# Moving the U tiles of a short-convolution layer 32 bytes along in SBUF

## The chip, the cores and the metric

The kernel runs on one core of a Trainium2 chip. The metric is the device time of one launch in microseconds (us). Three runs of the kernel before took 773.32, 773.86 and 774.14 us, with a median of 773.86.

## What is computed

One layer of an encoder trunk (the reference has depth 1, so only its first mixer runs), for 1024 positions of 1024 channels, in float32:

```python
u = rms_norm(h, pre_norm)                        # 1024 x 1024
z, bg, cg, v = split(u @ w_in, 4)                # w_in: 1024 x 8192, four parts of 2048
y = bg * causal_dwconv(cg * v, conv_w) * silu(z) # three taps along the positions
m = y @ w_out                                    # w_out: 2048 x 1024
h = h + rms_norm(m, post_norm)
```

Nearly all of the work is the two matrix products, `u @ w_in` and `y @ w_out`.

## The kernel before

**Precision.** A float32 operand is split into a high part (rounded to the fp32r format) and a low part, what is left of it. A product is then three matmuls per block of the inner dimension: low weights by high input, high weights by low input, high weights by high input (lines 821 to 823, 1425 to 1427 and 1839 to 1841). Every matmul has 128 x 128 weights, loaded just before it, and streams a moving operand of 512 or 256 columns past them. Throughout this document the *moving* operand is the one named first after the arrow in a profile row: `px<-u_d,wdh` streams `u_d` past the weights `wdh` into the PSUM bank `px`.

**Fewer products.** The 2 x 2 blocks of each product are combined in Strassen's manner (Winograd's form): seven block products, named a to g, in place of eight. Three of them, b, f and g, are for most chunks split once more in the same way, into seven smaller products a' to g' whose moving operands have 256 columns. The whole first product runs over 32 pairs p (16 chunks c of 128 output channels, two pairs each); the deep form is used for b in chunks 2 to 15 (14 chunks), for f in 2 to 14 (13), and for g in 2 to 13 (12) (`by_seven`, line 767).

**Where tiles lie.** SBUF is handed out by pools, in the order in which the kernel opens them, one after another and in steps of 32 bytes per partition. In the program before, the pools on which this case turns lie as follows (addresses within a partition):

| pool | what it holds | size of a tile | first address | rest by 64 |
|---|---|---|---|---|
| `up` | the U tiles: 7 slots, used in turn for `u_a` to `u_g`, `xb`, and in the output stage for `ou_*`, `oy_*`, `oA_*`, `oB_*`, `ox_*` | 16,384 | 3,136 | 0 |
| `pages` | 32 pages: raw weights, their sums, their high and low parts (`w*h`, `w*l`, `dw*`), snapshots | 2,048 | 117,824 | 0 |
| `tmp` (opened when the head is done) | `gpad`, 4,104 bytes, takes 4,128 | | 183,360 | 0 |
| `tmp` | `cv`, then 18 slots `u?*_deep` | 4,096; 2,048 | 187,488; 191,584 | 32 |

All slices that a matmul reads begin at multiples of 512 bytes from the start of their tile, so a slice has the same rest by 64 as its tile. So the moving operands of products a to g, and of a', b', e' and f' (slices of `u_b`, `u_f`, `u_g`), begin on a 64-byte line. Those of c', d' and g' are tiles of their own (`deep_split`, line 1347; names `ub?h_deep`, `ub?l_deep` and so on) and begin 32 bytes past one. This comes of the 4,104 bytes of `gpad` alone. All weights begin on a 64-byte line: in the first product they are pages, in the output stage (`out_mm`, line 1831, and `small_mm`, line 1924) they are U tiles, like the moving operands there.

**Order.** Every instruction after the head is recorded first, put into an order by a list scheduler (`Plan.arrange`, line 388) with its own costs for the engines, corrected by a table of hand-set numbers (`PLAN`, line 28), and then issued engine by engine. The order doesn't depend on addresses. TensorE runs the products in the order of `slots` (line 1620): for a pair, c, e, d, the next pair's a, with the deep products of b, f and g between them. ScalarE rounds the high parts and takes snapshots of banks (`snap`, line 827), VectorE makes the low parts and adds, GpSimd makes the sums of weight blocks, SyncE issues the DMAs. After about 615 us comes the output stage: products a to g of `y @ w_out`, 512 columns each but for b and f, which are done in seven of 256 columns; then the last norm and the stores.

All instructions of the profile stand under one line, 252, that of the helper that issues them; tile names tell them apart.

Of the kernel before, what the change touches and what calls it, by code (L numbers as in the profile page):

```python
# [11 lines left out]
F32 = mybir.dt.float32  # L12
# [187 lines left out]
class Op:  # L200

    __slots__ = ("lock", "order", "base", "move", "others", "lead", "est", "engine", "name", "args", "kw", "n", "needs", "feeds", "dur", "lat", "waits", "late", "tiles", "news", "start", "ideal", "pos", "soft")


class Engine:
# [409 lines left out]
def kernel(  # L615
# [35 lines left out]

    const = plan.pool(ctx.enter_context(tc.tile_pool(name="const", bufs=1)), 1)
    small = plan.pool(ctx.enter_context(tc.tile_pool(name="small", bufs=2)), 2)
    up = plan.pool(ctx.enter_context(tc.tile_pool(name="up", bufs=7)), 7)
    pages = plan.pool(ctx.enter_context(tc.tile_pool(name="pages", bufs=PAGES)), PAGES)
    psum = plan.pool(ctx.enter_context(tc.tile_pool(name="psum", bufs=8, space=bass.MemoryType.PSUM)), 8, "psum")
    dram = plan.pool(ctx.enter_context(tc.tile_pool(name="dram", bufs=1, space=bass.MemoryType.DRAM)), 1, "dram")
# [1408 lines left out]
```

## Time and profile before

| | |
|---|---|
| median of three runs | 773.86 us |
| the profiled execution's own time | 772.83 us |
| its span, first to last instruction | 771.0 us |
| mean granted TensorE clock | 0.998 |
| TensorE busy (PE) | 762.2 us, 4320 matmuls |
| VectorE busy (DVE) | 673.9 us |
| ScalarE busy (ACT) | 458.8 us |
| GpSimd busy (POOL) | 462.2 us |

A matmul is pipelined: its recorded duration reaches into the next one. What a matmul costs in a dense row of matmuls is therefore the distance from its start to the next one's start. In the chain of waits, a piece such as "x6" is six matmuls in a row, and its length is the sum of six such distances.

### The profile page before, as it was taken

The numbers are of one execution on the slowest core, as the hardware profiler recorded it, in microseconds if no ns is written. First come the engines' busy times: TensorE is split into PE (matmuls) and PEld (weight loads), VectorE is DVE, ScalarE is ACT, GpSimd is POOL, SyncE is SP. The second block draws the span as 40 slices with busy tenths as digits, with TensorE's granted clock in tenths as the row PEclk, the third lists the DMA queues.
The fourth block names the chain that finished last, engine by engine and source line by source line (L and its number), as shares of the span: only waits on it lengthen the run. The fifth ranks groups of instructions, "written<-read, shape, count | busy, mean of one in ns | idle before, by whom it ended". The sixth has DMA issues, their size and how long they took to land.

```text
span 771.0 us, 12816 instructions
## 1 busy us (share of the span) xinstructions
PE 762.2 (99%) x4320; PEld 669.6 (87%) x4320; DVE 673.9 (87%) x1022; ACT 458.8 (60%) x880; POOL 462.2 (60%) x416
## 2 busy tenths in 40 slices
PE   8999999999999999999999999999999999999996
PEld 7888889898889898888888898988888889889885
DVE  6899988989988978989999989798999898877993
ACT  7765678575656565556556565556653656564831
POOL 2519997889575778696789777584739100600321
PEclk9999999999999999999999999999999999999999
DMA  9222325243333547576858474927465998666842
GB/s 318 66 56 82 119 85 152 101 126 131 97 116 96 171 111 209 126 191 158 239 137 254 116 215 107 249 84 213 122 180 174 335 367 293 197 218 206 274 150 109
DMA packets 117137, 130.11 MB, mean 169 GB/s; under 512 B 7320, under 2 KB 74704, under 8 KB 116944
## 3 DMA queue, kind: packets, MB, share of 16 engines
q1 hardware_dynamic: 112560, 120.77, 49.0%
q0 software_dynamic: 4352, 8.39, 7.1%
q8 instruction: 34, 0.56, 0.3%
q14 instruction: 31, 0.25, 0.1%
q10 hardware_dynamic: 160, 0.14, 0.0%
HBM read 101.74 MB, written 44.30 MB: 189 GB/s over the span
## 4 chain that ended last, share of the span: by engine, by line
PE 98%; DVE 1%; DMA 0%; ACT 0%; POOL 0%; issue 0%; POOLq 0%; ACTq 0%
PE px L252 39%; PE pv L252 15%; PE po_x L252 11%; PE px2b L252 5%; PE px2f L252 4%; PE px2g L252 3%; PE po_v L252 3%; PE pp L252 3%; PE pv2b L252 3%; PE pv2f L252 2%; PE pf_x L252 1%; PE pb_x L252 1%; PE py2b L252 1%; PE pv2g L252 1%; PE py L252 1%; PE pf_v L252 1%
## 5 line engine op out<-in xcount | busy, mean ns | idle before, releaser
L252 PE MATMUL px<-u_d,wdh 128*128 128x512 f32 x248 | 76.8, 390 | 0.0
L252 PE MATMUL px<-u_a,wah 128*128 128x512 f32 x248 | 76.7, 390 | 0.0
L252 PE MATMUL pv<-u_e,weh 128*128 128x512 f32 x248 | 76.7, 390 | 0.0
L252 PE MATMUL px<-u_c,wch 128*128 128x512 f32 x248 | 76.6, 390 | 0.0
L252 ACT COPY beside<-raw 128x512 f32<-128x512 f32 x67 | 39.6, 591 | 31.8 <-DVE wal L252 11.0
L252 PEld LDWEIGHTS px<-u_d,wdh 128*128 128x128 f32 x248 | 46.6, 188 | 9.1
L252 PEld LDWEIGHTS px<-u_c,wch 128*128 128x128 f32 x248 | 46.7, 188 | 9.0
L252 PEld LDWEIGHTS px<-u_a,wah 128*128 128x128 f32 x248 | 46.7, 188 | 8.9
L252 PEld LDWEIGHTS pv<-u_e,weh 128*128 128x128 f32 x248 | 46.6, 188 | 8.9
L252 DVE SCALAR_TENSOR_TENSOR cv<-gpad,cw,cv 128x1024 f32<-128x1024 f32 x32 | 49.7, 1554 | 3.4 <-ACT cv L252 3.3
L252 POOL TENSOR_TENSOR sf<-raw,sc 128x512 f32<-128x512 f32 x30 | 44.5, 1482 | 10.9 <-DVE sc L252 6.0
L252 PE MATMUL px<-u_d,wdl 128*128 128x512 f32 x124 | 48.7, 393 | 0.0
L252 PE MATMUL px<-u_a,wal 128*128 128x512 f32 x124 | 48.7, 393 | 0.0
L252 PE MATMUL px<-u_c,wcl 128*128 128x512 f32 x124 | 48.5, 392 | 0.0
L252 PE MATMUL pv<-u_e,wel 128*128 128x512 f32 x124 | 48.5, 391 | 0.0
L252 POOL TENSOR_TENSOR sc<-se,raw 128x512 f32<-128x512 f32 x25 | 36.5, 1460 | 19.0 <-DVE se L252 10.0
L252 ACT COPY sna<-px 128x512 f32<-128x512 f32 x30 | 17.6, 586 | 49.4 <-PE px L252 47.7
L252 POOL TENSOR_TENSOR raw<-raw,raw 128x512 f32<-128x512 f32 x31 | 44.8, 1446 | 3.3 <-DVE se L252 1.9
L252 POOL TENSOR_TENSOR rs_post<-ve_post,minus_half 128x1 f32<-128x1 f32 x7 | 5.4, 784 | 68.1 <-DVE ve_post L252 68.1
L252 POOL TENSOR_TENSOR se<-raw,raw 128x512 f32<-128x512 f32 x22 | 33.1, 1504 | 17.7 <-DMA raw<-in_sc_w_in 5.7
L252 DVE TENSOR_TENSOR wcl<-sc,wch 128x512 fp32r<-128x512 f32 x31 | 31.6, 1020 | 2.6 <-ACT wch L252 2.6
L252 DVE TENSOR_TENSOR sna<-px2b,sna 128x256 f32<-128x256 f32 x56 | 23.2, 413 | 11.9 <-PE px2b L252 11.9
(486 smaller groups left out, 2637.1 us busy)
## 6 DMA issues: line engine op xcount, KB each, us to landing
raw<-in_sc_w_in SPq DMA_DIRECT2D x128, 256.0 KB, 4.6
y_d<-cv SPq DMA_DIRECT2D x16, 512.0 KB, 3.1
s_d<-s SPq DMA_DIRECT2D x32, 256.0 KB, 4.8
t_d<-in_sc_w_out POOLq DMA_DIRECT2D x16, 512.0 KB, 8.2
tb<-in_sc_w_out SPq DMA_DIRECT2D x16, 256.0 KB, 3.0
t_d<-in_sc_w_out SPq DMA_DIRECT2D x16, 256.0 KB, 4.5
t_d<-t_d SPq DMA_DIRECT2D x16, 256.0 KB, 4.5
s<-y_d SPq DMA_DIRECT2D x16, 256.0 KB, 4.7
```

The source lines that it names most:

```text
L252: getattr(engine, name)(*(self.plain(a) for a in args), **{k: self.plain(a) for k, a in kw.items()})
```

## The change

Two pools of one tile of 32 bytes are opened, one ahead of `up` and one behind it. Nothing reads or writes their tiles.

```diff
+def edge(ctx, tc, name):
+
+    ctx.enter_context(tc.tile_pool(name=name, bufs=1)).tile([128, 8], F32, tag=name, name=name)
...
     small = plan.pool(ctx.enter_context(tc.tile_pool(name="small", bufs=2)), 2)
+    edge(ctx, tc, "edge_u")
     up = plan.pool(ctx.enter_context(tc.tile_pool(name="up", bufs=7)), 7)
+    edge(ctx, tc, "edge_w")
     pages = plan.pool(ctx.enter_context(tc.tile_pool(name="pages", bufs=PAGES)), PAGES)
```

The U tiles then begin at 3,168, 32 bytes past a 64-byte line. The pages and all that lies behind them move by 64 bytes in all, so that their rest by 64 stays: 0 for pages and `gpad`, 32 for `cv` and the deep tiles. No instruction is added, removed or moved to another place in the order.

## The prediction

> **What bounds the kernel.** I read the page first: busy shares, the slices, the chain.
>
> ```profile
> PE 762.2 (99%) x4320; PEld 669.6 (87%) x4320; DVE 673.9 (87%) x1022; ACT 458.8 (60%) x880; POOL 462.2 (60%) x416
> PE   8999999999999999999999999999999999999996
> PE 98%; DVE 1%; DMA 0%; ACT 0%; POOL 0%; issue 0%; POOLq 0%; ACTq 0%
> ```
>
> TensorE is busy in every slice and makes up 98% of the chain that ends last. Nothing else sets the time, so the question is what one matmul costs. The busy time doesn't tell that, since recorded durations overlap; the distance from start to start does. The chain of waits gives it, in pieces (start, length, what, how many matmuls). Here is one stretch of the first product, and the place where the output stage begins:
>
> ```profile
> 303.70 2.75 PE pv L252 x12
> 306.45 0.71 PE pv2b L252 x6
> 307.16 0.72 PE pv2f L252 x6
> 307.88 0.71 PE px2b L252 x6
> 308.59 0.71 PE px2f L252 x6
> ...
> 312.05 0.70 PE px2b L252 x6
> 312.75 0.70 PE pv L252 x6
> 313.45 0.72 PE px L252 x6
> 314.17 0.72 PE px2g L252 x6
> ```
>
> ```profile
> 602.03 2.72 PE pv L252 x12
> 604.75 0.71 PE pv2b L252 x6
> 605.46 0.71 PE px2b L252 x6
> 606.17 2.75 PE px L252 x12
> ...
> 615.09 21.76 PE po_x L252 x96
> 636.85 2.87 PE pb_x L252 x24
> ```
>
> Two things are to be seen. A matmul of 512 columns costs 226.7 ns in a long run (21.76 us for 96; 2.72 for 12). One of 256 costs 120 ns in some pieces (0.72 for six) and 116.7 ns in others (0.70). The timeline tells which are which, around another such place:
>
> ```profile
> 127.29 0.28 PE L252 MATMUL px2b<-ubgh_deep,dwb 128*128 128x256 f32 x1
> ...
> 127.99 0.28 PE L252 MATMUL pv<-ufgh_deep,dwf 128*128 128x256 f32 x1
> ...
> 128.69 0.28 PE L252 MATMUL px<-u_g,dwg0l 128*128 128x256 f32 x1
> ...
> 129.41 0.28 PE L252 MATMUL px2g<-u_g,dwg0l 128*128 128x256 f32 x1
> ```
>
> The twelve from 127.29 to 128.69 us stream deep tiles: 1.40 us, 116.7 ns each. The six from 128.69 to 129.41 stream `u_g`: 0.72 us, 120 ns each. Both have 256 columns and weights out of pages. What differs is the moving tile: the deep tiles begin 32 bytes past a 64-byte line, `u_g` on one. So the kernel before already contains, in small, what the change does to the U tiles, and there the matmul is 3.3 ns cheaper. The groups by form say the same by durations, of matmuls and of weight loads (count, busy, mean ns):
>
> ```profile
> L252 PE MATMUL px2b<-ubgh_deep,dwb 128*128 128x256 f32 x56 | 12.1, 279 | 0.0
> L252 PE MATMUL py2b<-u_b,dwb0h 128*128 128x256 f32 x56 | 10.7, 283 | 0.0
> L252 PEld LDWEIGHTS px2b<-ubgh_deep,dwb 128*128 128x128 f32 x56 | 9.5, 188 | 0.5
> L252 PEld LDWEIGHTS py2b<-u_b,dwb0h 128*128 128x128 f32 x56 | 8.7, 192 | 0.0
> ```
>
> 279 against 283 ns for the matmul, 188 against 192 for the load that runs beside it. Both streams are shorter where the moving tile lies 32 bytes off the weights' rest by 64, which looks like two reads getting in each other's way when they start alike. That is an argument from two numbers, not a proof.
>
> **The change, part by part.** It adds no instruction, wait or DMA and moves none past another. All it can do is change what an instruction costs that reads or writes a U tile.
>
> *Matmuls of 512 columns in the first product.* Their counts come from these groups, where the high weights are two of every three matmuls:
>
> ```profile
> L252 PE MATMUL px<-u_d,wdh 128*128 128x512 f32 x248 | 76.8, 390 | 0.0
> L252 PE MATMUL px<-u_g,wgh 128*128 128x512 f32 x56 | 17.3, 390 | 0.0
> L252 PE MATMUL pv<-u_f,wfh 128*128 128x512 f32 x40 | 12.3, 389 | 0.0
> L252 PE MATMUL py<-u_b,wbh 128*128 128x512 f32 x24 | 7.4, 390 | 0.0
> ```
>
> a, c, d and e have 248 each, so (4 x 248 + 56 + 40 + 24) x 1.5 = 1668, and the plain first pair has eight blocks of 12, 96: 1764. No matmul of 512 columns in this trace streams a tile 32 bytes off, so the gain is unknown. The bounds are nothing and the 4.2 ns that 1.39 in place of the rounded 1.40 us would give the short ones. The nearest row is the 256-column one: 120 - 106.7 = 13.3 ns stand above the 256 / 2.4 ns of the columns themselves, and 226.7 - 213.3 = 13.3 above 512 / 2.4 (2.4 columns a ns is an estimate: 256 more columns cost 226.7 - 120 = 106.7 ns). The same surcharge, independent of length, suggests the same relief. I take 3.3 ns: 1764 x 3.3 = 5.9 us.
>
> *Matmuls of 256 columns that stream U tiles in the first product.* Products a', b', e' and f' of 14 + 13 + 12 = 39 deep forms, six each: 4 x 6 x 39 = 936. `py2b` above has 56 x 1.5 = 84 = 14 x 6, as it should. 936 x 3.3 = 3.1 us, with bounds 2.3 and 3.9 (1.41 and 1.39 us for the twelve).
>
> *Deep tiles that follow U tiles.* At 307.88 and 308.59 they take 0.71 us for six, after U pieces, and at 312.05, after a product of 512 columns, 0.70. If no aligned piece is left, these fall to 0.70: one piece in each of 39 deep forms, 0.01 each, 0.4 us; bounds 0 and 0.8.
>
> *The output stage.* There the weights are U tiles as well. Five products of 96 matmuls of 512 columns and two of 168 with 256 give 816. Weights and moving tile go along together, so their rests by 64 remain alike, as they are today at 226.7 and 120 ns. If two reads that start alike are what costs, nothing changes. Bounds: a gain of 816 x 3.3 = 2.7 us if only the moving tile's start counts, and a loss of 816 x 4 = 3.3 if a shifted weight load is longer by the 4 ns that loads differ in today. The nearest row is today's equal rests, so I take 0.
>
> [...]
>
> *The first matmuls of 512 columns after short ones.* A piece of 12 takes 2.75 us after short pieces (606.17) and 2.72 after long ones (602.03). With eight such pieces in each of 13 chunks that is 104 x 0.03 = 3.1 us. Whether a shifted tile removes it can't be seen: 0 to 3.1 us, and I take 0, because at 606.17 it follows deep tiles that already lie 32 bytes off.
>
> *Writers of U tiles.* The rounding into `u_b` and into a deep tile cost the same:
>
> ```profile
> L252 ACT CAST u_b<-deepb 128x256 fp32r<-128x256 f32 x2 | 0.8, 407 | 0.4 <-PE py L252 0.3
> L252 ACT CAST ubch_deep<-deepb 128x256 fp32r<-128x256 f32 x2 | 0.7, 407 | 0.0
> ```
>
> 407 ns both; I count 0.
>
> *What is late next.* TensorE would run 1.2% faster. VectorE in the middle:
>
> ```profile
> 325.00:405.00 80.00, 80.00 (x480) 71.36 (x479) 72.39 (x107) 44.17 (x85) 60.94 (x58) 1.00 0.66 178
> ```
>
> 72.39 of 80 us is 90%, and becomes about 92%. It keeps up on the average, but has tight places. The tightest I found is a low part of weights, and the tightest that repeats a snapshot of a bank, each followed by the matmul that needs it:
>
> ```profile
> 419.01 0.68 DVE L252 TENSOR_TENSOR wdl<-beside,wdh 128x512 fp32r<-128x512 f32 x1
> ```
>
> ```profile
> 419.89 0.40 PE L252 MATMUL px<-u_d,wdl 128*128 128x512 f32 x1
> ```
>
> ```profile
> 298.20 0.59 ACT L252 COPY sna<-px 128x512 f32<-128x512 f32 x1 [3.44 <-PE px L252]
> ```
>
> ```profile
> 299.37 0.40 PE L252 MATMUL px<-u_c,wcl 128*128 128x512 f32 x1
> ```
>
> 0.20 us and 0.58 us are in hand. Matmuls 3.3 ns cheaper take 0.04 us out of the dozen between snapshot and use, which is nothing; the 0.20 us can be used up where VectorE runs for 0.20 / 0.012, some 17 us, without waiting for TensorE. I charge 0.4 us, with bounds 0 and 2.
>
> The sum is -5.9 - 3.1 - 0.4 + 0.4 = -9.0 us. Against the profiled execution's own 772.83 us that is 763.8. The median of the runs, 773.86, lies 1.03 higher, and it is what is forecast: 764.9.
>
> **The rivals.** *The moving start alone counts.* The output stage gains as well: 764.9 - 2.7 = 762.2. For it: the surcharge of 13.3 ns is as large there as in the first product. Against it: the shorter weight loads.
>
> *Only short matmuls gain.* A matmul of 512 columns leaves 227 ns for a load of 188, a short one only 120; the loads of the short ones overlap the next, and only they might suffer. Then 3.1 + 0.4 = 3.5 us go: 770.4. Against it: the equal surcharge.
>
> *No effect.* The deep tiles also lie elsewhere, above 191,584, the U tiles below 117,824, and the difference could be the region's. Then nothing changes: 773.9. Against it: seven U slots spread over 114,688 bytes show no difference among themselves. [...]
>
> *Slower: the long matmuls settle in a worse rhythm.* After short ones they run slow for half a piece:
>
> ```profile
> 300.76 0.39 PE L252 MATMUL px<-u_c,wcl 128*128 128x512 f32 x1
> ```
>
> From 299.37 to 300.76 are six, 231.7 ns each, 5.0 more than in the long run. Today this dies out. If a shifted tile held it, 1764 x 5.0 = 8.8 us come, 3.5 go: 779.2. It decides from 3.5 / 1764 = 2.0 ns on, a steady distance above 228.7 ns. For it: deep pieces after U pieces do hold their 0.71. Against it: that hold is still below 0.72.
>
> **How the numbers follow.** Forecast 0.43, moving start alone 0.22, short ones only 0.13, no effect 0.10, worse rhythm 0.12. About 0.2%, 1.5 us, is what a measurement of this kernel can tell from no change. Faster: 0.43 + 0.22 + 0.13 = 0.78; same 0.10; slower 0.12. The range takes in the first three cases: low, 762.2 less the 3.1 of the first long matmuls, 759.1; high, 770.4 and a little over for the feeders, 771.0.
>
> **What would show it.** Right: `po_x` still 21.76 us for 96, long pieces of `px` and `pv` in the first product at 2.68 for 12, all deep pieces at 0.70, loads of `py2b` at 188 ns. If `po_x` falls to 21.4, the moving start alone counts. If long pieces stay at 2.72 while short ones fall, the second rival is true; if `py2b` keeps 283 ns, the third. A piece above 2.74 in a long run is the fourth. What would make me wrong without any of these is a wait of TensorE on VectorE or a DMA that isn't in the chain today.

## The result, and the profile after

The changed kernel takes 779.61 us (median of six runs, 779.37 to 780.00), the kernel before 773.90 (six runs, 773.32 to 774.21). The ratio is 1.0075, with a 95% interval from 1.0062 to 1.0088: **slower by 5.7 us**, where 764.9, faster by 9.0, was forecast. The profiled execution took 779.58 us, its span is 777.8, its mean granted TensorE clock 0.999 (before: 772.83, 771.0 and 0.998).

The page of the changed kernel, first the busy times, then the shares of the chain that ends last:

```profile
PE 767.8 (99%) x4320; PEld 667.0 (86%) x4320; DVE 673.3 (87%) x1022; ACT 459.0 (59%) x880; POOL 461.4 (59%) x416
PE 98%; DVE 0%; DMA 0%; ACT 0%; POOL 0%; issue 0%; POOLq 0%; ACTq 0%
```

No new wait is there: TensorE is still 98% of the chain, with as many matmuls. So some of them must have become dearer. Two windows of 500 us, of before and then of after (time, then for each engine its busy time and instructions in the order PE, PEld, DVE, ACT, POOL, then clock, DMA share and GB/s), say so without any durations:

```profile
100.00:600.00 500.00, 500.00 (x2967) 445.00 (x2966) 446.80 (x681) 299.58 (x582) 371.28 (x336) 1.00 0.55 153
```

```profile
100.00:600.00 500.00, 500.00 (x2944) 439.84 (x2943) 442.65 (x675) 297.98 (x580) 366.86 (x336) 1.00 0.54 150
```

At the same clock, 23 matmuls fewer were started in the same time. VectorE had less to do per us, not more.

The chain of waits of the changed kernel, first in the plain first pair, where long pieces follow one another, then at the stretch of the first product and the place that the prediction showed of before:

```profile
74.14 2.80 PE pv L257 x12
76.94 2.80 PE px L257 x12
...
303.48 2.80 PE px L257 x12
306.28 0.70 PE px2f L257 x6
...
621.89 21.76 PE po_x L257 x96
```

Twelve matmuls of 512 columns take 2.80 us, after other long ones (76.94) as well as after short ones (303.48): 233.3 ns each, in place of 226.7. Of the short pieces of this stretch more are at 0.70 than before, and fewer at 0.72. The output stage is as it was, 21.76 us for 96. The groups by form show the same in recorded durations, of matmuls and of a weight load:

```profile
L257 PE MATMUL px<-u_d,wdh 128*128 128x512 f32 x248 | 78.0, 395 | 0.0
L257 PE MATMUL po_x<-ou_d,oy_d 128*128 128x512 f32 x96 | 21.9, 389 | 0.0
L257 PE MATMUL py2b<-u_b,dwb0h 128*128 128x256 f32 x56 | 10.6, 281 | 0.0
```

```profile
L257 PEld LDWEIGHTS py2b<-u_b,dwb0h 128*128 128x128 f32 x56 | 8.5, 188 | 0.0
```

`u_d` against `wdh` went from 390 to 395 ns, `ou_d` against `oy_d` did not move, `u_b` fell from 283 to 281, and its load from 192 to 188.

Summed over the trace, start to start, the matmuls of the two profiled executions account for the time:

| matmuls | count | before, us (mean ns) | after, us (mean ns) | difference |
|---|---|---|---|---|
| first product, U tiles, 512 columns | 1764 | 404.35 (229.2) | 412.32 (233.7) | +7.97 |
| first product, U tiles, 256 columns | 936 | 111.73 (119.4) | 110.75 (118.3) | -0.98 |
| first product, deep tiles, 256 columns | 702 | 82.44 (117.4) | 81.95 (116.7) | -0.49 |
| output stage, 256 columns | 336 | 40.31 (120.0) | 40.30 (120.0) | 0 |
| output stage, 512 columns | 479 | 108.63 (226.8) | 108.63 (226.8) | 0 |

The sum is +6.5 of the 6.8 us by which the span grew; the other 0.3 lie in the warm-up matmuls at the start (7.60 and 7.89 us). The mean of before is 229.2, not 226.7, mostly since pieces of 12 after short ones took 2.75 us; 13 early ones of more than 260 ns add another 1.3 us. After the change long pieces take 2.80 after long and short ones alike.

### The profile page after: what moved, and what is told of

Same layout as the page of the kernel before. It is cut to its first block, busy times and chain, and to the rows that moved or that the text cites. A ratio compares the mean times of both kernels' runs of the same rounds, so it can differ in the third digit from the quotient of the medians.

```text
span 777.8 us, 12816 instructions
## 1 busy us (share of the span) xinstructions
PE 767.8 (99%) x4320; PEld 667.0 (86%) x4320; DVE 673.3 (87%) x1022; ACT 459.0 (59%) x880; POOL 461.4 (59%) x416
## 4 chain that ended last, share of the span: by engine, by line
PE 98%; DMA 0%; DVE 0%; ACT 0%; POOL 0%; issue 0%; POOLq 0%; ACTq 0%
PE px L257 39%; PE pv L257 15%; PE po_x L257 11%; PE px2b L257 5%; PE px2f L257 4%; PE px2g L257 3%; PE pp L257 3%; PE po_v L257 3%; PE pv2b L257 3%; PE pv2f L257 2%; PE pf_x L257 1%; PE pb_x L257 1%; PE py2b L257 1%; PE py L257 1%; PE pv2g L257 1%; PE pf_v L257 1%
## 5 line engine op out<-in xcount | busy, mean ns | idle before, releaser
L257 POOL TENSOR_TENSOR se<-raw,raw 128x512 f32<-128x512 f32 x22 | 31.5, 1431 | 18.2 <-DMA raw<-in_sc_w_in 10.2
```

The source lines that it names most:

```text
L257: getattr(engine, name)(*(self.plain(a) for a in args), **{k: self.plain(a) for k, a in kw.items()})
```

## The experiments

Two words are used below. **Offset** is the address where the moving slice begins less the address where its weights begin, modulo 256 bytes (the expectations call it the distance). The whole kernel before has offset 0 for U tiles in both products and 32 for deep tiles. The change moved the U tiles by 32 and the pages by 64, so its offset is -32, that is 224, for U tiles in the first product, and still 0 in the output stage and 32 for deep tiles. **Time per matmul** is from start to start, steady, behind the first five of a piece.

The first theory was that only the offset counts; its rival was that the moving tile's own start counts.

### Both together

```diff
 up = plan.pool(ctx.enter_context(tc.tile_pool(name="up", bufs=7)), 7)
-edge(ctx, tc, "edge_w")
```

Against the changed kernel: U tiles and pages both begin 32 bytes past a multiple of 64.

> Only the edge ahead of the U tiles: U tiles and pages both begin 32 bytes past a 64-byte line, the deep tiles on one. Theory 1 (the distance between the starts of the moving tile and of the weights counts, by 64 bytes): U tiles against pages are equal again, so long matmuls return to 226.7 ns and short ones from U tiles to 120; deep tiles still differ from their weights by 32 and keep 116.7; time as before, 773.9 us. Theory 2 (the moving tile's own start counts): long matmuls stay at 233.3 ns, deep ones go to 120; about 780 us.

773.32 us (11 runs), ratio to before 1.0001 [0.9992, 1.0010]. The chain of this kernel, in the plain first pair and then in the deep stretch:

```profile
67.54 2.72 PE pv L257 x12
...
304.16 2.75 PE pv L257 x12
...
314.64 0.72 PE px2g L257 x6
```

All is as before, though every U tile lies where the change put it: 2.72 us for 12, not 2.80. Here the moving tile's own start does not count by itself, and neither does the weights', which has moved as well.

### Only the weights moved

```diff
-edge(ctx, tc, "edge_u")
 up = plan.pool(ctx.enter_context(tc.tile_pool(name="up", bufs=7)), 7)
 edge(ctx, tc, "edge_w")
```

U tiles stay where they were before, pages move by 32: offset 224, the change's own.

> Only the edge behind the U tiles: U tiles on a 64-byte line as before, pages (all weights of the first product) 32 bytes past one, deep tiles on one. Theory 1: weights and moving tiles differ by 32 everywhere in the first product, so it runs as with the change: long 233.3 ns, short about 117 to 118, about 779.6 us; the output stage (both U tiles) stays at 226.7. Theory 2: the moving starts of U tiles are those of before, so long ones cost 226.7, and deep ones go from 116.7 to 120: about 776 us.

779.48 us (one run), within 0.2 us of the changed kernel. The chain of this kernel at the same two places and at the output stage:

```profile
68.43 2.80 PE pv L257 x12
...
306.17 0.70 PE px2f L257 x6
...
621.78 21.76 PE po_x L257 x96
```

The loss of the change comes back without one U tile moved. The two experiments together show that the offset decides, at least between 0 (773.32 us) and 224 (779.48).

### Only the short products moved, slots padded by 128 bytes

```diff
+PAD = 128
+OFF = {'u_b': 32, 'u_f': 32, 'u_g': 32}
+def u_tile(name, dtype, pattern, **sizes):
+    at = OFF.get(name, OFF.get(name.split("_")[0], 0)) // 4
+    t = up.tile([P, 2 * KH * HB + PAD // 4], dtype, tag="u", name=name)
+    return t[:, at : at + 2 * KH * HB].rearrange(pattern, **sizes)
...
-    u = up.tile([P, 2, KH, HB], F32R, tag="u", name=f"u_{i}")
+    u = u_tile(f"u_{i}", F32R, "p (z k l) -> p z k l", z=2, k=KH)
```

Against before; the other U tiles go through `u_tile` in the same way.

> u_b, u_f and u_g alone begin 32 bytes past a line (inside slots padded by 128 bytes); u_a, u_c, u_d, u_e, pages, deep tiles and the output stage as before. Theory 1: 936 short matmuls gain about 2 ns, as they did in the changed kernel, or up to 3.3; 180 long ones of b, f and g lose 6.6 ns, 1.2 us; the other long ones stay at 226.7 but for the first after short ones. 772 to 773.2 us. A rival (the slow rhythm is a state that spreads from any shifted tile to the long matmuls after it): long ones of a, c, d, e slow down as well, to 230 ns and more, 776 us or above.

777.68 us, ratio 1.0059 [1.0046, 1.0071], where 772 to 773.2 was expected. The padding itself spoilt it. Slots then follow one another by 16,512 bytes, which is 64 and a half times 256, so that every other slot has offset 128 in place of 0. That makes it an experiment of its own. The groups by form of this kernel, with tiles whose own rests by 64 are all 0:

```profile
L252 PE MATMUL px<-u_c,wch 128*128 128x512 f32 x248 | 77.6, 394 | 0.0
L252 PE MATMUL px<-u_a,wah 128*128 128x512 f32 x248 | 76.7, 391 | 0.0
L252 PE MATMUL po_x<-ou_c,oy_c 128*128 128x512 f32 x96 | 22.5, 395 | 0.0
L252 PE MATMUL po_x<-ou_d,oy_d 128*128 128x512 f32 x96 | 22.0, 390 | 0.0
```

`u_c` and `ou_c` against their weights have offset 128, `u_a` and `ou_d` have 0. Start to start they take 233.0 and 232.4 ns against 226.8 and 226.8. The product of `ou_a` uses two tiles, the first at offset 128 and the second at 0: 232.2 and 226.8 ns within one product. So neither rest by 64 nor rest by 128 tells the fast ones from the slow; in this kernel those at offset 0 modulo 256 take 226.8 ns and those at 128 from 232.2 to 233.0. By its time alone this run would suit the rival of a slow rhythm that spreads (776 us or more), but `u_a`, at offset 0 among shifted neighbours, stays at 226.8.

### A map of offsets

```diff
-OFF = {'u_b': 32, 'u_f': 32, 'u_g': 32}
+OFF = {'u_a': 16, 'u_c': 48, 'u_d': 64, 'u_e': 8, 'u_b': 16, 'u_f': 64, 'u_g': 8}
```

Against the kernel above. Here too the padding adds 128 to some offsets, so those that result are 16 (`u_a`), 64 (`u_d`, `u_f`), 136 (`u_e`, `u_g`), 144 (`u_b`) and 176 (`u_c`).

> A map in one run: u_a begins 16 bytes past a line, u_c 48, u_d 64, u_e 8, u_b 16, u_f 64, u_g 8, weights at 0. Theory 1 with a period of 64 bytes: u_d and u_f (64) behave as at 0, 226.7 and 120 ns; 16, 48 and 8 have values of their own. [...] A rival (the period is longer than 64): u_d and u_f differ from 226.7 and 120.

781.42 us (one run). At 512 columns, steady: about 231 ns at 16, 230 and 231 at 64, 233 to 234 at 136, 144 and 176. A period of 64 bytes would have given 226.7 at 64. The chain of this kernel in the plain first pair, with the pieces of `u_e`, `u_f` and `u_b`:

```profile
68.60 2.81 PE pv L252 x12
...
74.17 2.75 PE pv L252 x12
...
79.70 2.80 PE py L252 x12
```

None is at 2.72. Of the offsets in the kernels so far, only 0 gives 226.7 to 226.8 ns at 512 columns.

### Matmuls alone, by offset and length

The layer isn't computed; groups of 48 matmuls of one length and one offset run behind one another.

```python
for n, d in PLAN:
    for j in range(48):
        w = both[:, j % 8 * P : (j % 8 + 1) * P]
        at = 1024 + j % 8 * 512 + d // 4
        nc.tensor.matmul(ps[:, :n], w, both[:, at : at + n], start=True, stop=True)
```

> Matmuls alone, none of the layer is computed: runs of 48 with fp32r weights and moving tile in one SBUF tile, weights at a rest of 0, the moving start d bytes past the same rest by 256; 512, 384, 256 and 128 columns with d of 0, 32, 64, 128, 256, 8, 16, 96, 192, and 448, 320, 192 columns with d of 0 and 32. Theory 1 with a period of 256 bytes: d = 256 as d = 0; 512 columns 226.7 ns at 0 and 230 to 234 at any other d; 256 columns 120 at 0 and 116 to 119 at others. If the sign turns with the length, the other lengths show where; if the sign belongs to this kernel's order (short pieces between long ones), long runs here don't show it.

This kernel and the four other ones without the layer ran once each, at a granted clock of 1.00. The chain of this one; a name such as `n512d32q` gives columns and offset, and a 48th of a piece is the time per matmul, but for a dearer entry:

```profile
22.98 10.88 PE n512d0q L43 x48
...
42.20 5.75 PE n256d0q L43 x48
...
53.27 11.24 PE n512d32q L43 x48
...
72.99 5.65 PE n256d32q L43 x48
...
144.90 10.94 PE n512d256q L43 x48
...
175.25 11.25 PE n512d8q L43 x48
...
307.70 7.04 PE n320d0q L43 x48
...
330.01 7.04 PE n320d32q L43 x48
```

Steady times per matmul in ns:

| columns | 0 | 256 | 8 | 16 | 32 | 64 | 96 | 128 | 192 |
|---|---|---|---|---|---|---|---|---|---|
| 512 | 226.7 | 226.7 | 233.3 | 231.6 | 233.3 | 228.9 | 233.4 | 232.4 | 233.4 |
| 384 | 173.3 | 173.3 | 180.0 | 175.6 | 176.7 | 173.3 | 176.6 | 175.6 | 174.7 |
| 256 | 120.0 | 120.0 | 116.7 | 116.7 | 117.8 | 117.8 | 120.1 | 118.7 | 117.8 |

At 320 columns offsets 0 and 32 both take 7.04 us for 48, 146.7 ns each. At 448 columns they take 202.7 and 206.7 ns. So the sign of the effect depends on the length: an offset other than 0 helps at 256 columns (but for 96), 32 changes nothing at 320, and others than 0 cost from 384 on (but for 64 there). Two values lie outside what was expected: 228.9 at 64 and 120.1 at 96. The change's own offset, 224, is not among those that ran here. This is the step of the prediction that failed, outside any kernel: what an offset gives at 256 columns doesn't tell what it gives at 512.

### Long and short ones in turn

The layer isn't computed; twelve matmuls of 512 columns at offset a, then six of 256 at offset b, ten times.

```python
for j in range(18):
    n, d = (256, b) if j >= 12 else (512, a)
```

> Matmuls alone, none of the layer is computed: 12 of 512 columns, then 6 of 256, ten times, for pairs of distances (long, short) of 0/0, 0/32, 32/32, 32/0, 0/16, 0/64, 0/128. 0/0: 12 long ones at 2.75 us (the first six slow), 0/32: the same long ones, short ones at 0.70; 32/32: long ones 2.80. If short ones at some distance leave the long ones after them alone, their 12 take 2.72.

The chain of this kernel, long pieces of three pairs and one short piece (a name gives the offsets of the long and of the short ones):

```profile
30.52 2.75 PE long0s0q L44 x12
...
96.17 2.80 PE long32s32q L44 x12
98.97 0.70 PE short32s32q L44 x6
...
166.26 2.72 PE long0s16q L44 x12
```

Of long and short ones together: 3.460 us at 0 and 0, 3.447 at 0 and 32, 3.500 at 32 and 32, 3.513 at 32 and 0, 3.433 at 0 and 16, 3.467 at 0 and 64, 3.480 at 0 and 128. The pieces of the whole kernels are found again, 2.75 and 2.80. With the long ones at 0, their 12 take 2.75 us when the short ones are at 0 or 32 and 2.76 when they are at 64 or 128, in place of 2.72 when they are at 16. That slow start, which the prediction charged at 0 to 3.1 us, changes with the offset of the short ones alone.

### Only the short products moved, slots padded by 256 bytes

```diff
-PAD = 128
+PAD = 256
...
-ident = const.tile([P, P], F32, tag="ident", name="ident")
-idle = small.tile([P, P], F32, tag="idle", name="idle", bufs=1)
+ident = hp.tile([P, P], F32, tag="ident", name="ident")
+idle = hp.tile([P, P], F32, tag="idle", name="idle")
```

Against the first padded kernel. The offset is now 32 for `u_b`, `u_f` and `u_g`, and 0 for all other U tiles. `ident` and `idle` move into the pool of the head to make room.

> The third experiment with slots padded by 256 bytes (the identity and the zeros of the warm-up move into the pool of the head to make room), so that u_a, c, d, e and the output stage's tiles keep a distance to their weights that is a multiple of 256 bytes; u_b, u_f, u_g alone are 32 bytes off. Theory 1 with a period of 256 bytes: long ones of a, c, d, e and of the output stage back at 226.7 (but for the first after short ones); 936 short ones gain about 2 to 3 ns, 180 long ones lose 6.6: 772 to 773. A rival, that shifted short ones leave the long ones after them in a slow rhythm: 775 or more.

772.46 us (11 runs), ratio to before 0.9989 [0.9980, 0.9998]. The chain of this kernel, in the plain first pair (the pieces of `u_d`, then `u_f`) and in the deep stretch:

```profile
70.64 2.72 PE px L252 x12
73.36 2.80 PE pv L252 x12
...
303.77 2.75 PE pv L252 x12
306.52 0.70 PE pv2b L252 x6
```

All short pieces of this stretch are at 0.70. Summed over the trace, the 936 short ones of U tiles fall by 2.22 us to 117.0 ns each, the deep ones by 0.25, and the 1764 long ones rise by 2.38. Of these, 228 stream `u_b`, `u_f` and `u_g` (the expectation counted 180 and left out the plain first pair); they go to 233.3 ns, which is 1.4 us. Most of the rest is TensorE waiting for VectorE:

```profile
557.26 0.72 PE L252 MATMUL px<-u_g,wgh 128*128 128x512 f32 x2 [0.21 <-DVE u_g L252]
```

The matmul ahead of it began at 556.65; 0.61 us pass where 0.23 are usual, until VectorE has made the low part of `u_g`. Three microseconds on, `u_c` waits for `wcl` in the same way; with the slower matmul behind each, the two places cost 0.8 us. In the profiled execution gains and losses cancel (its span is 771.1 us); over the runs 0.9 us are left.

### Own load or next load

The layer isn't computed. Weights or moving tile, or both, take turns between two starts 32 bytes apart.

```python
odd = j % 2 * 8
dw = odd if kind in ("wts", "own", "next") else 0
dm = odd if kind in ("mov", "own") else 8 - odd if kind == "next" else 0
```

With "own" a matmul is at offset 0 to its own weights and 32 or -32 to the ones loaded while it runs; with "next" it is the other way about.

> Matmuls alone, none of the layer is computed: runs of 48 with 512 and with 256 columns in which weights, moving tile or both step back and forth by 32 bytes from one matmul to the next. Runs named own: each matmul's moving start lies like its own weights and 32 bytes off the next ones; runs named next: the reverse. If the load of the next weights, which runs beside a matmul, meets its moving stream, own costs 233 ns at 512 columns and 117 at 256, next 226.7 and 120. If the distance to the matmul's own weights counts, it is the other way round. If only the starts of successive moving tiles count, own and next are alike, and the run named wts equals the run named same.

The chain of this kernel:

```profile
23.36 10.88 PE n512same L45 x48
34.24 11.27 PE n512wts L45 x48
...
56.63 11.21 PE n512own L45 x48
67.84 11.13 PE n512next L45 x48
```

"own" and "next" are both slow, 233.8 and 231.6 ns. An offset of 0 to the matmul's own weights isn't enough, and neither is one to the next weights. Which pair of starts decides stays open, and one thing is gained: with weights in turn and moving starts fixed ("wts") it is 235.0, so successive moving starts alone aren't what counts. With moving starts in turn and weights fixed ("mov") it is 231.7. At 256 columns, where own was expected at 117 and next at 120 or the other way round, both take 118.4 ns (same 120.0, wts 116.7, mov 120.0).

### Long ones at 0, short ones elsewhere

The layer isn't computed; the kernel of long and short ones in turn, with a at 0 and b at 4, 8, 12, 16, 24, 48, 192 and 240.

> Matmuls alone, none of the layer is computed: 12 of 512 columns at distance 0, then 6 of 256 at a distance of 4, 8, 12, 16, 24, 48, 192 or 240 bytes, ten times. At 16 the 18 take 3.433 us as before. [...]

For 12 and 6 together, in us: 3.460 at 4, 3.467 at 8, 3.440 at 12, 3.433 at 16, 3.460 at 24 and at 48, 3.427 at 192, 3.433 at 240. The chain of this kernel, the best:

```profile
234.64 2.72 PE long0s192q L44 x12
237.36 0.71 PE short0s192q L44 x6
```

There is no order by size: at 12 the short ones are at their fastest (0.700) and the long ones slow (2.740), at 4 the short ones are slow (0.736) and the long ones fast (2.724).

### The best of these in the layer

```diff
-OFF = {'u_b': 32, 'u_f': 32, 'u_g': 32}
+OFF = {'u_b': 192, 'u_f': 192, 'u_g': 192}
...
+if kw["tag"] == "ub":
+    pool, (p, k, n) = self.pool, self.args[0]
+    if not pool.deep:
+        pool.deep = [pool.pool.tile([p, 18 * k * n + 40], self.args[1], tag="ub", name="ubs"), 40]
+    t, at = pool.deep
+    pool.deep[1] += k * n
+    self.made = t[:, at : at + k * n].rearrange("p (k n) -> p k n", k=k)
+    return self.made
```

Against the kernel with slots padded by 256 bytes. The deep tiles become slices of one tile that begins 160 bytes further on, so that all short matmuls of the first product are at 192. Two more small tiles move into the pool of the head.

> As the fifth experiment on the whole kernel, but u_b, u_f, u_g and the deep tiles all begin 192 bytes past the rest of their weights by 256, the distance at which matmuls alone took 3.427 us for 12 long and 6 short ones (3.460 at 0, 3.447 at 32). If that carries over: some 104 pieces of long ones after short ones lose their slow start, 104 x 0.028 = 2.9 us; 936 short ones go from 120 to 118, 1.9 us; 702 deep ones from 117.2 to 118, 0.5 us more; 180 long ones of b, f, g lose 6.6 ns, 1.2 us. Sum -3.1: about 770.3. If the slow start comes from the long matmuls themselves, 773.

771.33 us (nine runs) beside 773.49 of the kernel before on the same chip: ratio 0.9972 [0.9962, 0.9982]. 2.2 us are gained, where 3.1 were expected. The chain of this kernel, with the pieces of `u_d` and `u_f` in the plain pair, then the deep stretch:

```profile
70.51 2.72 PE px L261 x12
73.23 2.80 PE pv L261 x12
...
303.17 2.72 PE pv L261 x12
305.89 0.71 PE pv2b L261 x6
```

The long pieces after short ones have lost their slow start, 2.72 in place of 2.75. Over the trace the long ones fall by 1.07 us (those of `u_a`, `u_c`, `u_d` and `u_e` lose 2.4, and the 228 that stream `u_b`, `u_f` and `u_g` at 233.3 ns gain 1.4), and the 1638 short ones fall by 0.79 (193.38 for 111.73 + 82.44). The span is shorter by 1.8.

### The padding alone

```diff
-OFF = {'u_b': 32, 'u_f': 32, 'u_g': 32}
+OFF = {}
```

Against the first kernel with slots padded by 256 bytes.

> The fifth experiment without its offsets: slots of U tiles padded by 256 bytes and the identity and zeros in the pool of the head, every distance a multiple of 256 bytes as before (deep tiles 32). Theory 1 with a period of 256 bytes: all matmuls as before, 773.4 us, so that what the fifth experiment gained belongs to its offsets. If slots 16,640 bytes apart matter by themselves, the time differs.

773.14 us, ratio 0.9996 [0.9987, 1.0005]. The wider slots and the moved tiles `ident` and `idle` are worth nothing, so the gains of the two kernels with offsets don't come of them. That the deep tiles became slices of one tile, and that two further small tiles moved, was not tried alone.

### Narrower weight loads

The layer isn't computed; groups of 48 as above, with weights of 128, 96, 64 and 32 columns.

```diff
-w = both[:, j % 8 * P : (j % 8 + 1) * P]
+w = both[:, j % 8 * P : j % 8 * P + c]
```

> Matmuls alone, none of the layer is computed: runs of 48 with 512 and 256 columns, with weights of 128, 96, 64 and 32 columns (so that the load of the next weights reads for a shorter time), at distances of 0, 32 and 128 bytes. If the two streams meet while the load reads, what distance 32 adds at 512 columns (233.3 - 226.7 = 6.6 ns) and takes off at 256 (120 - 117.8 = 2.2) shrinks with the load, to about a quarter at 32 columns (1.7 and 0.5), and the surcharge of 13.3 ns may shrink as well. If the start alone counts, whatever reads beside it, 6.6 and 2.2 stay at every width.

The chain of this kernel (`w96` is the weights' width):

```profile
24.55 10.88 PE n512d0w128q L42 x48
35.43 11.20 PE n512d32w128q L42 x48
...
57.78 11.04 PE n512d0w96q L42 x48
68.82 10.88 PE n512d32w96q L42 x48
```

Neither expectation held. The load takes 188, 161, 134 and 108 ns at the four widths. At 512 columns offset 32 adds 6.6, -3.3, 0.9 and 1.1 ns to offset 0, at 256 columns -2.2, 0.6, 5.7 and 4.0. With weights 96 wide it turns round: offset 0 takes 230.0 ns and 32 takes 226.7. So the width of the weights alone changes which of the two offsets is the faster, and an offset of 0 is nothing special in itself. That this is the load's doing is not shown: narrower weights also make the matmul's output narrower.

## Why the prediction was wrong, point by point

**What bounds the kernel** was right: TensorE's matmuls are the chain before and after, and the time is a sum of times per matmul.

**Matmuls of 512 columns in the first product** is the step that failed. They were to lose 3.3 ns each, 5.9 us, and became dearer by 4.5 on average (229.2 to 233.7), 8.0 us: from it alone come 13.9 us of the 15.8 between 763.8, the forecast for the profiled execution, and its 779.58. (1764 x 3.3 is 5.8; the 5.9 comes with 3.33.) The step went from 256 to 512 columns because both stand 13.3 ns above their columns' own time at offset 0, "the same surcharge, independent of length, suggests the same relief". The surcharge is the same there; the relief is not. In the matmuls alone offset 32 leaves 117.8 - 106.7 = 11.1 ns at 256 columns, 13.3 at 320 (146.7 - 133.3) and 233.3 - 213.3 = 20.0 at 512. The equal surcharge at one offset told nothing of another offset. The same offset turns from a gain of 2.2 ns into a loss of 6.6. The bounds, nothing to 4.2 ns, excluded a loss without a reason, and only the fourth rival held one.

**The fourth rival** is what came: it gave 779.2, and 779.61 was measured; its test, a piece above 2.74 us in a long run, was met with 2.80. Its mechanism was half right. The steady time did move past the 228.7 ns from which it decides, but no slow start of the old kind was "held": the plain first pair of the changed kernel has 2.80 for 12 with no short one near, the matmuls alone have 233.3 at 32, and the old slow start of 231.7 ns comes or goes with the short ones' offset (2.75 us for 12 after short ones at 0, 2.72 after 16). That the time comes within 0.4 us is in part luck, since its two sizes were off against each other: 8.0 in place of 8.8 for the long ones, 1.5 in place of 3.5 for the short and deep ones.

**Matmuls of 256 columns that stream U tiles** gained 0.98 us, not 3.1. They were taken to copy the deep tiles, but these have offset 32, and the change gave the U tiles -32. In the kernel with U tiles of the short products at 32 they gained 2.22 us; there the long pieces beside them were mostly at 0 as well, so the sign isn't the only difference between the two. The rest by 64, with which the prediction worked, can't tell 32 from -32. The load of `py2b` fell to 188 ns as the test said; it foretold nothing of the long ones.

**Deep tiles that follow U tiles** gained 0.49, for 0.4. The rounding into `u_b` takes 407 ns, as before. **The output stage** stayed at 21.76 us, as forecast, and for the reason given: weights and moving tile went along together. That reason was the one right piece of mechanism: the first two experiments show that the relation of the two starts decides and neither start by itself. It speaks against the rival that the moving start alone counts: moving the weights alone would then have left the long matmuls at 226.7 ns, but they went to 233.3, and it cost 6.1 us (779.48 in one run, 773.36 before).

**What is late next** was not put to the test by the change, since TensorE got slower. The faster kernels test it. In the fastest, of `u_b`, `u_f`, `u_g` and the deep tiles at 192, the window from 100 to 600 us has the first row below, and the tightest place that the prediction named the other two:

```profile
100.00:600.00 500.00, 499.95 (x2980) 445.83 (x2979) 450.50 (x685) 301.07 (x585) 372.13 (x337) 1.00 0.55 154
```

```profile
418.15 0.68 DVE L261 TENSOR_TENSOR wdl<-beside,wdh 128x512 fp32r<-128x512 f32 x1
```

```profile
418.88 0.50 PE L261 MATMUL px<-u_d,wdl 128*128 128x512 f32 x1
```

TensorE starts 13 matmuls more than before in that time, and its records leave only 0.05 us of it empty. But at `wdl` the 0.20 us in hand are used up: the matmul starts 0.05 us behind VectorE's end, 0.28 us behind the one ahead of it where 0.12 are usual, and its own slot takes 0.335 us in place of 0.233, 0.26 us in all. The kernel with the short products at 32 loses 0.25 us there and 0.8 at `u_g` and `wcl`. So the place was named rightly, and the 0.4 us charged for a gain of 9 look too little: in that profiled execution more than 1 us went at a gain of about 1. What a gain of 9 would have cost wasn't seen.

**No effect, and short ones only** are excluded by the table above. In the matmuls alone, too, 48 of 512 columns take 11.24 us at offset 32, and 11.25 at 8, against 10.88 at 0.

**What stays open** is why the relation of the two starts matters. Shown are that the offset decides (226.7 ns at 0 and 233.3 at 32, 512 columns), that 256 is as good as 0 (226.7), that the width of the weights changes which of 0 and 32 is the faster (226.7 and 233.3 ns at 128 wide, 230.0 and 226.7 at 96), and that the offset to the own or to the next weights alone doesn't explain it (233.8 and 231.6). No run shows what happens between the two streams.

## What to carry to other kernels

Where every matmul has its own weight load, look at the address of the moving slice less that of its weights, modulo 256, before moving either tile or padding a slot: slots padded by 128 bytes made a kernel 5.2 us slower than the same slots padded by 256 (777.68 and 772.46). For matmuls of 512 columns with 128-wide weights start from offset 0 (226.7 ns here, 228.9 to 233.4 at the others tried), for 256 columns try others (120.0 at 0, 116.7 to 118.7 at all others tried but 96 and 256), and measure each length and width, since the sign turned here. Where the matmuls get cheaper, look again at the tight places of the engines that feed them (0.26 us went at `wdl` in the fastest kernel). A gain seen at one size of an operation is no evidence for another size, not even for its sign (offset 32 gains 2.2 ns at 256 columns and costs 6.6 at 512), and a bound of zero needs a reason of its own.

## What the runs showed of the hardware that was not expected

- With a load of 128-wide weights for each matmul, offset 0 costs 13.3 ns above 2.4 columns a ns (the estimate from the difference of 512 and 256 columns) at 256, 320, 384 and 512 columns (16.0 at 448: 202.7 ns), and other offsets between 10.0 (116.7 at 256) and 20.1 (233.4 at 512).
- Matmuls of 128 columns take 5.31 us for 48, steady 111.7 ns each, at every offset tried, and those of 192 columns take 111.7 ns too at 0 and 32: something other than the columns sets the time there, and which it is isn't shown.
- The width of the weights matters even where the load, of 108 to 188 ns, is shorter than the 227 ns from matmul to matmul. At 512 columns offset 0 takes 226.7, 230.0, 230.0 and 231.7 ns with weights 128, 96, 64 and 32 wide: narrower weights make the matmul slower at that offset. At 256 columns they make it faster at offset 0, from 120.0 to 113.3 ns at 64 and 32 wide.
- The offset of short matmuls changes the time of the long ones behind them: 2.747 us for twelve after short ones at offset 0, 2.720 after short ones at 16 or 192, with the long ones' own addresses unchanged.
